# SwiGLU_1's first half in staircase order, with the first root's Newton steps on GpSimd

## The chip, the cores and the metric

The kernel runs as one program on one core of a Trainium2 chip. The metric is the device time of one execution in microseconds (us), as the median of several runs.

## The reference, cut to what matters

One decoder layer on 256 tokens of width 2048, in float32: SwiGLU_1, a mixer, SwiGLU_2, each behind an RMSNorm whose output is scaled and shifted by vectors that come from the conditioning `c` (adaLN).

```python
cond = jax.nn.silu(c)
mod = cond @ ada_w[l] + ada_b[l]                       # 2048 x 18432
sh1, sc1, gt1, ... = jnp.split(mod, 9, axis=-1)
h = rmsnorm(x, norm_g[l, 0]) * (1 + sc1) + sh1
x = x + 0.5 * gt1 * ((silu(h @ wg) * (h @ wu)) @ wd)   # wg, wu 2048 x 5632
...
```

The change touches what comes first: the norm of x, the first columns of `mod`, and the products `h @ wg` and `h @ wu` for 28 of the 44 tiles of 128 features.

## The kernel before, in words

**Weights.** All products are made of 128x128 weight tiles, which lie in HBM in the order of their use, eight to a block of 512 KB. `Stream.next` hands out the next tile. At the first tile of a block, `Stream.block` starts the block's load on SP's queue (`wraw`), ScalarE (ACT) rounds it to float32r (`whi`), and VectorE (DVE) subtracts to get the rest (`wlo`). A product in float32 is then three products in float32r: high weight by high h, high weight by low h, low weight by high h. In the first half those are the three matmuls of `three`, each with 256 columns. `raw`, `hi` and `lo` have four buffers each; every fifth block's `wraw` has a buffer of its own (`more`).

**The columns of mod.** One column of 128 outputs of `mod` is a row of 1 MB of `ada_w` (`adat`, or `adaf` for the first four), multiplied by silu(c) and summed by one DVE instruction (L257). The first two columns are done in halves (`first_col`, L683). h of contraction step k (128 of the 2048 inputs) needs two columns, scale and shift of k, and then `modulate_one` makes the high part of h on ACT and the low part on DVE, both in the tile `hs`. `Stream.next` calls `ada_col` at the pace of the table RATE (columns per block), and `ada_need` forces those that are still missing when a k is first used.

**The first half.** `gate_up_first` works on 28 pairs f; a pair is the gate tile and the up tile of one 128-wide slice of features, which share a PSUM bank of 512 columns. The pairs form groups of 8, 8, 8 and 4. Eight banks are all there is. CHUNKS splits the 16 steps of k into 0 to 1, 2 to 7 and 8 to 15, and every group goes through one chunk before the next begins. In each chunk group 0 leads: its eight pairs stand in eight banks and take the first LEAD steps k by k, so that each h is used sixteen times before the next is needed; the rest goes pair by pair. At the end of a chunk `evacuate` takes the bank: after the first chunk ACT copies it to an SBUF tile `acc` (L577), after the second DVE adds it to `acc` (L579), and after the last DVE adds gate and up (`tg`, `tu`, L582 and L583), ACT does the silu, DVE the product, and both split the result into `hid` (L497).

**The start.** Warm-up matmuls on zeros (`zp`), 32 transposes of x (`px`, copied to `x` by ACT), the squares of x on ACT, then the reciprocal root on DVE: a guess by bit shift and two Newton steps (`rsqrt`, L281 to L289). DVE spreads the two roots over `frb`, two matmuls make them a row over all partitions (`nrow`), and ACT copies it. Then h of k=0 can be made. The tiles of the start live in the pool `early`, which is closed ahead of the first half; the tiles `acc` and `hid` come from the pool that takes its place in SBUF, where the third and fourth column (`adaf`) are still to be summed.

Each engine runs its own instructions strictly in the order in which the build put them; the build's scheduler moves instructions of different steps past each other, and `tc.issue_after` binds it.

Of the kernel before, what the change touches and what calls it, by code (L numbers as in the profile page):

```python
# [30 lines left out]
GR = 24  # L31
NEG = -1e30

RATE = ((0, 0.5), (24, 0.34), (56, 0.45), (68, 0.06), (112, 0.5), (168, 0.38), (264, 0.1), (280, 0.25), (408, 0.125))
N_BIG, N_GDN = 3, 3
N_FIRST = 4
AHEAD = 4
N_WARM = (10, 7)
TILE_US = 0.35
HIDX = 3  # L40
MORE = True
# [9 lines left out]
MAGIC = 0x5F3759DF  # L51
# [37 lines left out]
class Stream:  # L89


    def __init__(self, nc, w, raw, hi, lo):
        self.nc, self.w, self.raw, self.hi, self.lo = nc, w, raw, hi, lo
        self.order = []
        self.more = None
        self.h = self.l = self.last = None
        self.owed, self.side, self.quiet = 0.0, lambda: None, False
        self.tc, self.hold, self.held = None, None, []
        self.first = []
        self.late, self.owing = False, []  # L100

    def settle(self):
# [4 lines left out]
    def behind(self, later=True):  # L107
# [2 lines left out]
            self.hold = self.held.pop(0)  # L110
        return nullcontext() if self.hold is None else self.tc.issue_after(self.hold)

    def block(self, b):

        raw, hi, lo = self.raw, self.hi, self.lo
        if self.more is not None and b % 5 == 4:
            raw = self.more
        r = raw.tile([P, WB * P], F32, name="wraw")
        self.last = self.nc.sync.dma_start(r, self.w[b]).ins
        self.h = hi.tile([P, WB * P], F32R, name="whi")  # L120
        self.cast = self.nc.scalar.copy(self.h, r).ins  # L121
        return r, lo

    def next(self, mat, k, n, width=1):
        i = len(self.order)
        if i % WB == 0:
            nc = self.nc
            b = i // WB
            r, lo = self.first.pop(0) if self.first else self.block(b)
            self.l = lo.tile([P, WB * P], F32R, name="wlo")  # L130
            pace = [r_ for r_ in RATE if r_[0] <= b][-1][1]
            with self.behind():
                nc.vector.tensor_tensor(self.l, r, self.h.bitcast(F32), ALU.subtract)  # L133
# [13 lines left out]
def layer_kernel(ctx: ExitStack, tc: tile.TileContext, xrow, c, adaw, cols, cst, w, out, order, dbg=None):  # L147
    nc = tc.nc
    V, A, G, PE = nc.vector, nc.scalar, nc.gpsimd, nc.tensor
# [26 lines left out]
    W = Stream(nc, w, raw, hi, lo)  # L176
# [3 lines left out]
    x = keep.tile([P, KD, T], F32, name="x")  # L180
# [4 lines left out]
    ep = early.enter_context(tc.tile_pool(name="early", bufs=1))  # L185
# [6 lines left out]
    one = ep.tile([P, P], F32, name="one")  # L192
# [168 lines left out]
    def modulate_one(j, g1, sh, r, weave=True):  # L361

        t = pt("ht")
        hl, hh, tt = (run(j, LO), run(j, HI), turns(t)) if weave else (plain[:, j, LO], plain[:, j, HI], t)
        V.scalar_tensor_tensor(t, x[:, j], g1, r, ALU.mult, ALU.mult)
        if j % 2:
            A.activation(t, t, AF.Identity, bias=sh)
            A.copy(hh, tt)  # L368
            return V.tensor_tensor(hl, tt, hh.bitcast(F32), ALU.subtract)
        else:  # L370
            with tc.issue_after(W.cast) if W.first else nullcontext():
                A.activation(hh, tt, AF.Identity, bias=sh)  # L372
            return V.scalar_tensor_tensor(hl, tt, sh, hh.bitcast(F32), ALU.add, ALU.subtract)

    def gains(which, m_sc, j, n):
# [173 lines left out]
    def gate_up_first(fs, hp):  # L549

        r = first_row
        for j in range(KD):
            ada_done[0, j] = lambda j=j: modulate_one(j, gains(0, 1, j, 1), mod[:, j : j + 1], r)
        W.hold, W.held = None, [ada_done[0, 0]().ins]
        groups = [fs[i : i + 8] for i in range(0, len(fs), 8)]
        chunks = list(zip(CHUNKS[:-1], CHUNKS[1:]))
        acc, hids = {}, []

        def three(ps, f, s, k, k0, k1):
            o = ps[:, s * T : (s + 1) * T]  # L560
            wh, wl = W.next(("gu"[s], 0), k, f)
            first, last = k == k0, k == k1 - 1
            skip = s == 1
            PE.matmul(o, wh, part(k, HI), start=first and s == 0, stop=False, skip_group_check=skip)  # L564
            PE.matmul(o, wh, part(k, LO), start=False, stop=False, skip_group_check=skip)  # L565
            PE.matmul(o, wl, part(k, HI), start=False, stop=last, skip_group_check=skip)  # L566

        turn = [0]

        def bank():  # L570
            turn[0] += 1
            return psn(turn[0], "pgu")

        def evacuate(ps, f, ci):
            if ci == 0:
                acc[f] = hp.tile([P, 2 * T], F32, name="acc", tag="hid")
                A.copy(acc[f], ps)  # L577
            elif ci < len(chunks) - 1:
                V.tensor_add(acc[f], ps, acc[f])  # L579
            else:  # L580
                tg, tu = pt("tg"), pt("tu")
                V.tensor_add(tg, ps[:, :T], acc[f][:, :T])  # L582
                V.tensor_add(tu, ps[:, T:], acc[f][:, T:])  # L583
                hids.append(swi(tg, tu, hp))

        for ci, (k0, k1) in enumerate(chunks):
            for gi, grp in enumerate(groups):
                if gi == 0 and LEAD[ci]:
                    pb = {f: bank() for f in grp}
                    ks = k0 + LEAD[ci]  # L590
                    for k in range(k0, ks):
                        ada_need(0, k)
                        for f in grp:
                            for s in range(2):
                                three(pb[f], f, s, k, k0, k1)
                    for f in grp:
                        for k in range(ks, k1):
                            ada_need(0, k)
                            for s in range(2):
                                three(pb[f], f, s, k, k0, k1)  # L600
                        evacuate(pb[f], f, ci)
                else:
                    for f in grp:
                        pf = bank()
                        for k in range(k0, k1):
                            ada_need(0, k)
                            for s in range(2):
                                three(pf, f, s, k, k0, k1)
                        evacuate(pf, f, ci)
        return hids  # L610

    def ffn(which, m_gt, early=None):
# [41 lines left out]
    hold = None  # L654
    for kind, i in (("x", 0), ("x", 1), ("c", 0), ("c", 1), ("x", 2), ("x", 3), ("c", 2), ("c", 3)):
        with nullcontext() if hold is None else tc.issue_after(hold):
            if kind == "c":
                hold = cond(i)
            else:
                t, q = divmod(i, 2)  # L660
# [8 lines left out]
        with tc.issue_after(hold):  # L669
            return A.copy(x[:, 2 * i : 2 * i + 2], px.rearrange("p (a t) -> p a t", a=2))  # L670

    for i in range(4):
        features(i)
    fv = ep.tile([P, 2], F32, name="fv")

    def first_col(i, q):

        hf = slice(q * D // 2, (q + 1) * D // 2)
        m, j = ada_seq[i]
        col = m * KD + j  # L680
        part = ep.tile([P, 1], F32, name=f"part{i}")
        t = first_ada[i][:, hf]
        parts[i] = V.tensor_tensor_reduce(t, t, cs[:, hf], 1.0, L("adab", col, 1) if q == 0 else parts_[i], ALU.mult, ALU.add,  # L683
                                          part if q == 0 else mod[:, col : col + 1]).ins
        if q == 0:
            parts_[i] = part
        return parts[i]

    parts, parts_ = {}, {}
    first_col(0, 0)  # L690
    V.tensor_tensor(fv, ss[:, :, 0], ss[:, :, 1], ALU.add)
    V.tensor_scalar(fv, fv, 1.0 / D, EPS, ALU.mult, ALU.add)
    fy = rsqrt(fv, [P, 2], "n")
    frb = ep.tile([P, 2, P], F32, name="frb")
    pr = psf("nrow")
    for t in range(2):
        V.tensor_scalar(frb[:, t], one, fy[:, t : t + 1], None, ALU.mult)
        nr = PE.matmul(pr[:, t * P : (t + 1) * P], frb[:, t], ident, start=True, stop=True)
    first_row = tmp.tile([P, T], F32, name="nrow", bufs=1)
    hold = A.copy(first_row, pr[:, :T]).ins  # L700
    for i in range(4, KD // 2):
# [722 lines left out]
```

## Time and profile before

| | us |
|---|---|
| three runs | 1949.29, 1952.88, 1954.36 |
| median | 1952.88 |
| the profiled execution | 1954.36 |
| its span, first to last instruction | 1952.6 |
| PE busy | 1902.9 (97%) |
| DVE busy | 1557.3 (80%) |
| ACT busy | 1035.5 (53%) |
| POOL (GpSimd) busy | 57.0 (3%) |
| matmuls of the first half, first to last start | 22.8 to 337.0 |

A row of the timeline has the start in us from the span's start, the duration, the engine, the source line, the operation, output<-input by the program's names, the shapes and a count; in brackets stands the idle time of the engine ahead of it and what ended that. PEld are weight loads, which run beside the matmuls. Matmuls are pipelined, so the time of one is the distance from start to start and not its duration.

### The profile page before, as it was taken

How to read it: one execution, taken by the hardware profiler on the slowest of the kernel's cores; microseconds unless marked ns; L12 is line 12 of the kernel's file. 1: busy time of each engine (PE TensorE's matmuls, PEld its weight loads, DVE VectorE, ACT ScalarE, POOL GpSimd, SP SyncE). 2: the span in 40 equal slices, each digit the busy share in tenths (PEclk: the TensorE clock that was granted, in tenths of full speed). 3: DMA queues.
4: the chain of work that ended last, by engine and by line, in shares of the span. 5: the costliest groups of instructions: out<-in, count | busy, mean ns of one | idle time of the engine just before them, and what ended most of it. 6: DMA issues, size and time to landing. Idle time of an engine off the chain costs nothing.

```text
span 1952.6 us, 33709 instructions
## 1 busy us (share of the span) xinstructions
PE 1902.9 (97%) x13087; PEld 1776.3 (91%) x13087; DVE 1557.3 (80%) x2415; ACT 1035.5 (53%) x1645; POOL 57.0 (3%) x55
## 2 busy tenths in 40 slices
PE   8999999999999999999999999999999999999998
PEld 6999999998999988889989998889999999999997
DVE  6999978989999997889978979886766656565654
ACT  6544554433454446857657655565554445555553
POOL 0000000000000120000000002000000000000011
PEclk8999999999999999999999999999999999999999
DMA  9989867999999986685566658676777665555553
GB/s 369 359 321 349 300 221 254 398 381 376 356 353 342 347 317 218 251 302 205 203 239 236 211 215 315 226 258 249 255 249 239 201 200 203 201 200 202 200 202 119
DMA packets 129490, 519.58 MB, mean 266 GB/s; under 512 B 18217, under 2 KB 21545, under 8 KB 111153
## 3 DMA queue, kind: packets, MB, share of 16 engines
q1 hardware_dynamic: 129330, 517.42, 72.7%
q8 instruction: 103, 1.69, 0.3%
q14 instruction: 57, 0.47, 0.1%
HBM read 512.89 MB, written 4.47 MB: 265 GB/s over the span
## 4 chain that ended last, share of the span: by engine, by line
PE 76%; DVE 11%; DMA 5%; issue 4%; ACT 3%; SPq 0%; DVEq 0%; ACTq 0%
PE pd L482 14%; PE pg L478 10%; PE pu L478 10%; PE pd L483 7%; PE pu L479 5%; PE pg L479 5%; PE pgu L566 5%; PE pgu L565 5%; PE pgu L564 5%; DVE wlo L133 4%; DMA adat<-in_ada_dram 3%; DVE adat L257 2%; PE pp L758 2%; PE pp L759 2%; PE pp L760 2%
## 5 line engine op out<-in xcount | busy, mean ns | idle before, releaser
L133 DVE TENSOR_TENSOR wlo<-wraw,whi 128x1024 fp32r<-128x1024 f32 x674 | 821.1, 1227 | 242.7 <-ACT whi L121 241.3
L121 ACT CAST whi<-wraw 128x1024 fp32r<-128x1024 f32 x674 | 700.1, 1047 | 509.3 <-PE pd L482 166.5
L482 PE MATMUL pd<-hid,whi 128*128 128x512 f32 x1408 | 461.8, 382 | 0.0
L483 PE MATMUL pd<-hid,wlo 128*128 128x256 f32 x1408 | 384.6, 273 | 2.6 <-DVE wlo L133 2.4
L257 DVE CUSTOM_DVE_ANT_0 adat<-adat,cs,colt 128x2048 f32<-128x2048 f32 x140 | 329.5, 2354 | 40.9 <-DMA adat<-in_ada_dram 40.8
L478 PE MATMUL pg<-hs,whi 128*128 128x512 f32 x912 | 302.1, 382 | 2.5 <-DVE shc L429 2.5
L478 PE MATMUL pu<-hs,whi 128*128 128x512 f32 x912 | 302.2, 382 | 0.0
L482 PEld LDWEIGHTS pd<-hid,whi 128*128 128x128 f32 x1408 | 266.0, 189 | 36.5
L483 PEld LDWEIGHTS pd<-hid,wlo 128*128 128x128 f32 x1408 | 270.3, 192 | 5.4 <-DVE wlo L133 5.3
L564 PE MATMUL pgu<-hs,whi 128*128 128x256 f32 x896 | 245.3, 277 | 6.2 <-ACT hs L368 6.2
L479 PE MATMUL pu<-hs,wlo 128*128 128x256 f32 x912 | 249.3, 273 | 0.0
L479 PE MATMUL pg<-hs,wlo 128*128 128x256 f32 x912 | 248.9, 273 | 0.0
L566 PE MATMUL pgu<-hs,wlo 128*128 128x256 f32 x896 | 245.2, 278 | 2.4 <-DVE wlo L133 2.4
L565 PE MATMUL pgu<-hs,whi 128*128 128x256 f32 x896 | 246.8, 277 | 0.0
L478 PEld LDWEIGHTS pg<-hs,whi 128*128 128x128 f32 x912 | 172.4, 189 | 26.7 <-ACT whi L121 2.7
L478 PEld LDWEIGHTS pu<-hs,whi 128*128 128x128 f32 x912 | 172.4, 189 | 23.7
L758 PE MATMUL pp<-hs,whi 128*128 128x256 f32 x656 | 188.9, 289 | 1.5 <-ACT hs L372 1.5
L760 PE MATMUL pp<-hs,wlo 128*128 128x256 f32 x656 | 182.7, 278 | 1.1 <-DVE wlo L133 1.1
L759 PE MATMUL pp<-hs,whi 128*128 128x256 f32 x656 | 182.5, 278 | 0.0
L564 PEld LDWEIGHTS pgu<-hs,whi 128*128 128x128 f32 x896 | 172.3, 193 | 6.9 <-ACT hs L368 6.6
L479 PEld LDWEIGHTS pu<-hs,wlo 128*128 128x128 f32 x912 | 175.0, 192 | 1.3 <-DVE wlo L133 1.2
L479 PEld LDWEIGHTS pg<-hs,wlo 128*128 128x128 f32 x912 | 175.1, 192 | 0.4
(337 smaller groups left out, 2583.6 us busy)
## 6 DMA issues: line engine op xcount, KB each, us to landing
wraw<-in_w_dram SPq DMA_DIRECT2D x674, 512.0 KB, 4.3
adat<-in_ada_dram SPq DMA_DIRECT2D x140, 1024.0 KB, 7.4
xr<-in_xr_dram SPq DMA_DIRECT2D x4, 512.0 KB, 5.1
adaf<-in_ada_dram SPq DMA_DIRECT2D x4, 512.0 KB, 8.7
adaf<-in_ada_dram SPq DMA_DIRECT2D x2, 1024.0 KB, 11.3
xd<-x SPq DMA_DIRECT2D x4, 512.0 KB, 5.0
rw<-rowd SPq DMA_DIRECT2D x16, 128.0 KB, 6.7
x<-xd SPq DMA_DIRECT2D x4, 512.0 KB, 5.4
```

The costliest lines, as they stand in the source:

```text
L121: self.cast = self.nc.scalar.copy(self.h, r).ins
L133: nc.vector.tensor_tensor(self.l, r, self.h.bitcast(F32), ALU.subtract)
L257: V.tensor_tensor_reduce(t, t, cs, 1.0, L("adab", q, 1), ALU.mult, ALU.add, mod[:, q : q + 1])
L478: PE.matmul(ps, wt[0], both, start=(k == 0), stop=False)
L479: PE.matmul(ps[:, T:], wt[1], part(k, HI), start=False, stop=(k == KD - 1))
L482: PE.matmul(ps, wt[0], act.rearrange("p q (a b) -> p q b a", a=2), start=first, stop=False)
L483: PE.matmul(ps[:, :T], wt[1], woven(act[:, 0]), start=False, stop=last)
L564: PE.matmul(o, wh, part(k, HI), start=first and s == 0, stop=False, skip_group_check=skip)
L565: PE.matmul(o, wh, part(k, LO), start=False, stop=False, skip_group_check=skip)
L566: PE.matmul(o, wl, part(k, HI), start=False, stop=last, skip_group_check=skip)
L758: PE.matmul(pp[i][:, :T], wh, hh, start=(k == 0), stop=False)
L760: PE.matmul(pp[i][:, :T], wl, hh, start=False, stop=(k == KD - 1))
```

## The change

It changes four things.

1. The order of the first half. PIECES replaces CHUNKS and LEAD. An entry (g, k0, ks, k1) says: group g goes from k0 to k1, with k0 to ks pair-interleaved and the rest pair by pair. Group 0 now has three pieces (k 0; 1 to 3; 4 to 15), group 1 (0 to 1; 2 to 5; 6 to 15), group 2 (0 to 2; 3 to 9; 10 to 15), group 3 two (0 to 5; 6 to 15). The work is the same; there are 28 copies to `acc`, 24 adds to it where there were 28, and 28 closings.
2. The first root. The guess stays on DVE; the two Newton steps (ten instructions of 128x2) and the spreading to `frb` go to GpSimd, and the first half columns of `mod` stand behind the guess on DVE.
3. The start's order: six instead of four copies of transposes ahead of `nrow`, four instead of seven warm-ups after it, the first block's cast in two halves with h of k=0 between them, h of k=1 made like that of even k.
4. RATE has 0.43 up to block 70 instead of 0.5, 0.34 and 0.45.

```diff
-CHUNKS = (0, 2, 8, 16)
-LEAD = (2, 5, 5)
+PIECES = (
+    (0, 0, 1, 1), (1, 0, 2, 2), (2, 0, 3, 3), (0, 1, 4, 4), (1, 2, 6, 6), (3, 0, 0, 6),
...
-RATE = ((0, 0.5), (24, 0.34), (56, 0.45), (68, 0.06), ...
+RATE = ((0, 0.43), (70, 0.06), ...
-N_WARM = (10, 7)
+N_WARM = (10, 4)
...
     # Stream.block
-        self.cast = self.nc.scalar.copy(self.h, r).ins
+        with nullcontext() if b != 1 else self.tc.issue_after(self.lead):
+            one, *more = self.pieces(b)
+            h = self.h
+            self.cast = self.nc.scalar.copy(h[:, one], r[:, one]).ins
+            self.rest = [lambda q=q: self.nc.scalar.copy(h[:, q], r[:, q]) for q in more]
...
     # modulate_one
-        V.scalar_tensor_tensor(t, x[:, j], g1, r, ALU.mult, ALU.mult)
-        if j % 2:
+        with tc.issue_after(parts[1]) if W.first else nullcontext():
+            V.scalar_tensor_tensor(t, x[:, j], g1, r, ALU.mult, ALU.mult)
+        if j % 2 and j > 1:
...
     # gate_up_first
-        for ci, (k0, k1) in enumerate(chunks):
...
+        for g, k0, ks, k1 in PIECES:
+            grp = fs[8 * g : 8 * g + 8]
+            pb = {f: bank() for f in grp} if ks > k0 else {}
+            for k in range(k0, ks):
+                ada_need(0, k)
+                for f in grp:
+                    for s in range(2):
+                        three(pb[f], f, s, k, k0, k1)
+            for f in grp:
+                if f not in pb:
+                    pb[f] = bank()
+                for k in range(max(k0, ks), k1):
+                    ada_need(0, k)
+                    for s in range(2):
+                        three(pb[f], f, s, k, k0, k1)
+                evacuate(pb[f], f, k0, k1)
...
     # the start
-    for i in range(4):
+    for i in range(KD // 2 - 2):
         features(i)
...
-    first_col(0, 0)
-    fy = rsqrt(fv, [P, 2], "n")
+    V.tensor_scalar(fa.bitcast(I32), fv.bitcast(I32), 1, None, ALU.logical_shift_right)
+    guess = V.tensor_scalar(fy.bitcast(I32), fa.bitcast(I32), -1.0, float(MAGIC), ALU.mult, ALU.add)
+    with tc.issue_after(guess.ins):
+        first_col(0, 0)
+    for c0, c1, c2 in ((0.0, -0.1875, 0.5625), (64.0 / 9.0, -10.0 / 3.0, 5.0)):
+        G.tensor_tensor(fa, fy, fy, ALU.mult)
+        G.tensor_tensor(fa, fa, fv, ALU.mult)
...
+        G.tensor_tensor(fy, fy, fa, ALU.mult)
...
-        V.tensor_scalar(frb[:, t], one, fy[:, t : t + 1], None, ALU.mult)
+        G.tensor_scalar(frb[:, t], one, fy[:, t : t + 1], None, ALU.mult)
...
-    W.first.append(W.block(0))
+    with tc.issue_after(hold):
+        W.first.append(W.block(0))
```

How the instructions move, at three places. First PE at the start, from the row of roots (`nrow`) on; `px` are transposes of x, `zp` warm-ups. Before:

```order
L698 MATMUL nrow<-colt,frb 128x128 x2
L668 MATMUL px<-colt,xr 128x128 x8
L198 LDWEIGHTS zw
L198 MATMUL zp<-zw 128x512
L198 LDWEIGHTS zw
```

Now:

```order
L720 MATMUL nrow<-colt,frb 128x128 x2
L675 MATMUL px<-colt,xr 128x128 x4
L210 LDWEIGHTS zw
L210 MATMUL zp<-zw 128x512
L210 LDWEIGHTS zw
L210 MATMUL zp<-zw 128x512
L210 LDWEIGHTS zw
L210 MATMUL zp<-zw 128x512
L210 LDWEIGHTS zw
L210 MATMUL zp<-zw 128x512
L675 MATMUL px<-colt,xr 128x128 x4
L579 MATMUL pgu<-hs,whi 128x256 x2
```

The last four transposes now stand behind the warm-ups and right ahead of the first products; before, all eight stood ahead of the seven warm-ups.

Second ACT, from the casts of the first blocks to the copies of group 0's banks into `acc`, with h of k=1 (`hs`) among them; `whi` are the casts of the blocks in their order. Before:

```order
L121 CAST whi_329<-wraw_327 128x1024
L121 CAST whi_359<-wraw_357 128x1024
L367 ACTIVATE ht_322<-ht_322,mod_126 128x256
L368 CAST hs_127<-ht_322 128x2x128
L577 COPY acc_390<-pgu_252 128x512
L121 CAST whi_409<-wraw_407 128x1024
L577 COPY acc_392<-pgu_253 128x512
```

Now:

```order
L131 CAST whi_377<-wraw_375 128x1024
L131 CAST whi_415<-wraw_413 128x1024
L592 COPY acc_319<-pgu_254 128x512
L592 COPY acc_321<-pgu_255 128x512
L592 COPY acc_323<-pgu_256 128x512
L592 COPY acc_325<-pgu_257 128x512
L592 COPY acc_327<-pgu_258 128x512
L592 COPY acc_329<-pgu_259 128x512
L592 COPY acc_331<-pgu_260 128x512
L592 COPY acc_333<-pgu_261 128x512
L385 ACTIVATE hs_127<-ht_409,mod_126 128x2x128
L131 CAST whi_448<-wraw_446 128x1024
```

Group 0's eight copies have moved ahead of h of k=1. In the built program the first of them waits for DVE's total of the fourth column (besides PE's products), since its tile lies in the SBUF that the column was loaded to, and PE's first product of group 1 waits for that copy.

Third DVE, at the closing of group 0, whose pairs are now pgu_1885 to pgu_1892; `wlo_2659` and `wlo_2707` are the blocks 68 and 69 of the weights, and `wlo_2759`, thirteen small rows further on, is block 70. Before, with the pairs pgu_2216 to pgu_2223:

```order
L133 TENSOR_TENSOR wlo_2647<-wraw_2643,whi_2645 128x1024
L133 TENSOR_TENSOR wlo_2695<-wraw_2691,whi_2693 128x1024
L582 TENSOR_TENSOR tg_2586<-pgu_2216,acc_390 128x256
L583 TENSOR_TENSOR tu_2587<-pgu_2216,acc_390 128x256
L133 TENSOR_TENSOR wlo_2734<-wraw_2730,whi_2732 128x1024
L513 TENSOR_TENSOR tu_2587<-tu_2587,tg_2586 128x256
L582 TENSOR_TENSOR tg_2622<-pgu_2217,acc_392 128x256
L583 TENSOR_TENSOR tu_2623<-pgu_2217,acc_392 128x256
```

Now, from the closing of pgu_1888 (pair 3) on:

```order
L597 TENSOR_TENSOR tg_2646<-pgu_1888,acc_325 128x256
L514 TENSOR_TENSOR hid_2601<-tu_2596,hid_2601 128x256
L530 TENSOR_TENSOR tu_2626<-tu_2626,tg_2625 128x256
L598 TENSOR_TENSOR tu_2647<-pgu_1888,acc_325 128x256
L145 TENSOR_TENSOR wlo_2659<-wraw_2655,whi_2657 128x1024
L514 TENSOR_TENSOR hid_2631<-tu_2626,hid_2631 128x256
L530 TENSOR_TENSOR tu_2647<-tu_2647,tg_2646 128x256
L145 TENSOR_TENSOR wlo_2707<-wraw_2703,whi_2705 128x1024
L514 TENSOR_TENSOR hid_2652<-tu_2647,hid_2652 128x256
L269 ISA adat_2709,mod_126<-adat_2709,cs_86,colt_87 128x2048
L269 ISA mod_126 128x1
L597 TENSOR_TENSOR tg_2673<-pgu_1889,acc_327 128x256
```

Before, the blocks stood between the closing steps of single pairs, two ahead of the first; now blocks 68 and 69 stand behind those of four pairs, and block 70 behind those of all eight. In PE's order `wlo_2659` is first used in matmul 1640 of the half and `wlo_2759` in matmul 1684, counted from 0; the last products of pgu_1888 and pgu_1892 are matmuls 1631 and 1679.

More of the change, by code (lines that the diff above doesn't have):

```diff
@@ L132, in next @@
             with self.behind():
[L133 removed]
+                for q in self.pieces(b):
+                    nc.vector.tensor_tensor(self.l[:, q], r[:, q], self.h[:, q].bitcast(F32), ALU.subtract)
             self.settle()
@@ L371, in modulate_one @@
             with tc.issue_after(W.cast) if W.first else nullcontext():
-                A.activation(hh, tt, AF.Identity, bias=sh)
+                i = A.activation(hh, tt, AF.Identity, bias=sh)
+            if W.first:
+                W.lead = i.ins
+                with tc.issue_after(W.lead):
+                    W.rest.pop()()
             return V.scalar_tensor_tensor(hl, tt, sh, hh.bitcast(F32), ALU.add, ALU.subtract)
@@ L584, in evacuate @@
                 hids.append(swi(tg, tu, hp))
-        for ci, (k0, k1) in enumerate(chunks):
[L587 to L609, printed above, removed]
+        for g, k0, ks, k1 in PIECES:
[14 more added lines that the diff above has]
+                evacuate(pb[f], f, k0, k1)
         return hids
@@ L689, in layer_kernel @@
     parts, parts_ = {}, {}
-    first_col(0, 0)
     V.tensor_tensor(fv, ss[:, :, 0], ss[:, :, 1], ALU.add)
     V.tensor_scalar(fv, fv, 1.0 / D, EPS, ALU.mult, ALU.add)
-    fy = rsqrt(fv, [P, 2], "n")
+    fy = ep.tile([P, 2], F32, name="fy")
+    fa = ep.tile([P, 2], F32, name="fa")
+    V.tensor_scalar(fa.bitcast(I32), fv.bitcast(I32), 1, None, ALU.logical_shift_right)
[5 more added lines that the diff above has]
+        G.tensor_tensor(fa, fa, fv, ALU.mult)
+        if c0:
+            fb = ep.tile([P, 2], F32, name="fb")
+            G.tensor_scalar(fb, fa, c0 * c0, c0 * c1, ALU.mult, ALU.add)
+            G.tensor_tensor(fa, fa, fb, ALU.mult)
+            G.tensor_scalar(fa, fa, c2, None, ALU.add)
+        else:
+            G.tensor_scalar(fa, fa, c1, c2, ALU.mult, ALU.add)
+        G.tensor_tensor(fy, fy, fa, ALU.mult)
     frb = ep.tile([P, 2, P], F32, name="frb")
@@ L700, in layer_kernel @@
     hold = A.copy(first_row, pr[:, :T]).ins
-    for i in range(4, KD // 2):
+    for i in range(KD // 2 - 2, KD // 2):
         features(i)
```

16 lines of the change are left out of this document (10 added, 6 removed).

## The prediction

> **What bounds the kernel now.** I first asked for the busy time of each engine in four stretches, cut where the first half of SwiGLU_1 begins and ends. The columns are the stretch, its length, busy time and instructions of PE, PEld, DVE, ACT and POOL, the granted clock, the DMA share and GB/s.
>
> ```profile
> 0.00:22.70 22.70, 17.76 (x60) 10.43 (x61) 8.22 (x27) 13.98 (x26) 0.22 (x4) 0.78 0.91 351
> 22.70:106.40 83.70, 75.39 (x630) 74.06 (x628) 75.83 (x86) 47.68 (x68) 0.00 (x0) 0.96 0.91 355
> 106.40:337.40 231.00, 230.69 (x2062) 230.48 (x2063) 207.32 (x283) 112.17 (x151) 0.00 (x0) 1.00 0.79 290
> 337.40:1952.60 1615.20, 1579.02 (x10338) 1461.36 (x10336) 1265.93 (x2023) 861.67 (x1402) 56.81 (x51) 1.00 0.71 257
> ```
>
> TensorE bounds this kernel: from 106.4 to 337.4 it idles 0.3 us. What the change can win lies ahead of 106.4; what it can lose lies in all of the first half. The timeline of PE gives the pace and the waits.
>
> ```profile
> 299.81 0.28 PE L566 MATMUL pgu<-hs,wlo 128*128 128x256 f32 x1
> 310.53 0.28 PE L566 MATMUL pgu<-hs,wlo 128*128 128x256 f32 x1
> 32.35 0.49 PE L564 MATMUL pgu<-hs,whi 128*128 128x256 f32 x2 [3.89 <-ACT hs L368]
> 97.27 0.73 PE L564 MATMUL pgu<-hs,whi 128*128 128x256 f32 x4 [2.33 <-ACT hs L368]
> 106.47 0.38 PE L566 MATMUL pgu<-hs,wlo 128*128 128x256 f32 x1 [1.47 <-DVE wlo L133]
> ```
>
> Between the first two rows lie 96 matmuls, so one takes 0.1117 us, a weight tile (three of them) 0.335 and a block of eight tiles 2.68. The half has 896 tiles, 2688 matmuls; I number them from 0 in the order of PE. Matmuls 0 to 627 need 70.1 us at this pace and took 83.7, so 13.6 us are lost, in three waits (3.9, 2.3, 1.5) and the clock behind them. The clock is in the same matmuls by stretches of 2 us (busy PE, granted clock, DMA):
>
> ```profile
> 94.00:96.00 2.00, 0.93 (x9) 1.00 0.98 406
> 96.00:98.00 2.00, 0.73 (x5) 0.96 0.57 231
> 98.00:100.00 2.00, 2.00 (x12) 0.50 0.86 287
> 100.00:102.00 2.00, 2.00 (x14) 0.69 1.02 410
> ```
>
> After a wait of 2.33 us the clock is halved for about 3.4 us, which costs another 1.7. The Trainium skill, page "TensorE: Matmul & The Clock Gate", Part 1, has the clock fall only after an idle window of about 3.4 us; this trace differs, 2.33 us were enough. By the page the wait of 2.7 us below costs no clock, by the row it may cost 1.7; the sum is the same, since the longer wait right behind it takes that up.
>
> **The start.** Now the timeline up to the first product.
>
> ```profile
> 11.96 0.17 DVE L281 TENSOR_SCALAR rsa_n<-fv 128x2 int32<-128x2 int32 x1
> 12.09 1.28 DVE L683 CUSTOM_DVE_ANT_0 adaf<-adaf,cs,colt 128x1024 f32<-128x1024 f32 x1
> 17.08 0.48 DVE L697 TENSOR_SCALAR frb<-one,rsy_n 128x128 f32<-128x128 f32 x2
> 18.43 1.91 PE L668 MATMUL px<-colt,xr 128*128 128x128 f32 x8
> 18.68 0.37 ACT L700 COPY nrow<-nrow 128x256 f32<-128x256 f32 x1 [4.24 <-PE nrow L698]
> 18.95 1.57 ACT L670 COPY x<-px 128x512 f32<-128x512 f32 x3
> 20.14 2.96 PE L198 MATMUL zp<-zw 128*128 128x512 bf16 x7
> 21.80 0.56 ACT L372 ACTIVATE hs<-ht,mod 128x256 fp32r<-128x256 f32 x1
> 22.40 0.48 DVE L373 SCALAR_TENSOR_TENSOR hs<-ht,mod,hs 128x256 fp32r<-128x256 f32 x1 [2.83 <-ACT hs L372]
> ```
>
> Today `frb` is ready at 17.56, and h of k=0 (its high part, ACT at 21.80) ends 4.8 us later. The Newton steps now go to POOL, while DVE runs the four half columns (L683) back to back behind the guess. How POOL and DVE share is in the later rows where both work:
>
> ```profile
> 721.85 2.34 DVE L257 CUSTOM_DVE_ANT_0 adat<-adat,cs,colt 128x2048 f32<-128x2048 f32 x1
> 722.59 2.20 POOL L310 TENSOR_TENSOR sqacc<-sqacc,sq 128x256 f32<-128x256 f32 x1 [3.78 <-ACT sq L306]
> 724.18 1.69 DVE L133 TENSOR_TENSOR wlo<-wraw,whi 128x1024 fp32r<-128x1024 f32 x1
> 734.55 0.73 POOL L310 TENSOR_TENSOR sqacc<-sqacc,sq 128x256 f32<-128x256 f32 x1 [5.03 <-ACT sq L306]
> 750.93 0.12 POOL L961 MEMSET x<- 64x16 f32 x1
> 669.32 1.19 POOL L310 TENSOR_TENSOR sqacc<-sqacc,sq 128x256 f32<-128x256 f32 x1 [668.87 <-ACT sq L306]
> L310 POOLq MODIFY_POOL_CONFIG  x2: 11/11/11, 0.8 to 0.8; - x2
> ```
>
> Alone, POOL's add takes 0.73. The one at 722.59 meets a column on DVE and ends at 724.79, 0.6 after the column does, and DVE's next instruction takes 1.69 where it takes 1.14 otherwise: POOL waits out DVE's instruction, then DVE waits out POOL's. So each of the dependent Newton steps that meets a half column waits for its end: one step per half column. DVE: guess done at 12.3, four half columns of 1.21 and three holds of 0.3 end at 18.0. POOL has then done 4 of 10 steps; 6 more at 0.25 (a bare MEMSET is 0.12, the large add 0.73; I take a value near the small one, plus the step's own wait) and two `frb` at 0.35 (half the elements of the 0.73 row) end at 20.2, against 17.56: 2.7 later. The rest of the path grows as well. PE now has four transposes (0.95), four warm-ups (4 x 0.42) and then the last four transposes (0.95) between the row sum and h, and ACT copies both results (0.52 each) and casts half a block (0.5) ahead of h: 6.1 us behind `frb` instead of 4.8, 1.3 later. **Start: +4.0.** Lower end, with no holds and 0.2 a step: -1.4. Upper end, with 0.73 for each of the eight instructions left: +7.7.
>
> The Trainium skill, page "GPSIMD Engine Reference", "Instruction dispatch", adds about 6 us to the first call of a freshly loaded kernel, without a record. The first add here (669.32) shows nothing of it, and the two loading instructions stand at 0.8. By the page the sum would be up to 6 us higher, if the load starts only with the first step.
>
> **From h of k=0 to matmul 628.** I count from the row at 22.40; matmul 628 (the row at 106.47) comes 84.1 after it. The durations:
>
> ```profile
> 72.83 2.35 DVE L133 TENSOR_TENSOR wlo<-wraw,whi 128x1024 fp32r<-128x1024 f32 x2
> 75.10 2.35 DVE L257 CUSTOM_DVE_ANT_0 adat<-adat,cs,colt 128x2048 f32<-128x2048 f32 x1
> 77.37 0.08 DVE L257 DVE_READ_ACCUMULATOR2_ANT mod<- 128x1 f32 x1
> 38.64 2.05 ACT L577 COPY acc<-pgu 128x512 f32<-128x512 f32 x4
> 101.31 3.98 DVE L579 TENSOR_TENSOR acc<-pgu,acc 128x512 f32<-128x512 f32 x6 [0.38 <-PE pgu L566]
> 105.20 1.22 DVE L133 TENSOR_TENSOR wlo<-wraw,whi 128x1024 fp32r<-128x1024 f32 x1
> 219.15 0.41 DVE L582 TENSOR_TENSOR tg<-pgu,acc 128x256 f32<-128x256 f32 x1
> 219.49 0.41 DVE L583 TENSOR_TENSOR tu<-pgu,acc 128x256 f32<-128x256 f32 x1
> ```
>
> From start to start, a `wlo` block costs DVE 1.14, an ada column 2.27, an acc add 0.65, a 128x256 step 0.34; an acc copy costs ACT 0.5. In the staircase PE does group 0 with k=0 (matmuls 0 to 47) and then turns to group 1. All eight PSUM banks hold group 0, so matmul 48 waits for ACT's first acc copy. That copy also waits for the fourth ada column's total: the acc tiles lie where the closed pool `early` kept the third and fourth column. ACT's row no longer has h of k=1 ahead of the copies, as before. DVE reaches that total after h 0.4, two half blocks 1.2, two blocks 2.3, a column 2.27, g and ht 0.5, a block 1.14 and the column 2.27: 10.1. With the copy, PE goes on at 10.7; it had finished its 48 matmuls at 5.7. So the wait of 3.9 for k=1 becomes one of 5.0 for a bank, with 1.7 of clock behind it. The next h come in time. Two bursts of eight acc adds remain. Pair 0 of group 0 is done with matmul 389; then DVE has an add 0.65, a column 2.27, seven adds 4.55 and a block 1.2, 8.7 in all, while PE has 67 matmuls (7.5) until matmul 456 needs that block: 1.2. From there to the `wlo` that matmul 628 needs, DVE has 1.1 + 14.0 (three columns, five blocks, 1.5 of small steps) + 5.6 (eight adds, an h) + 1.2 = 21.9 and PE 172 matmuls, 19.2: 2.7. Together 10.7 + 1.7 + 580 x 0.1117 + 1.2 + 2.7 = 81.1 instead of 84.1. **This part: -3.0**, between -8.6 (clock and both bursts free) and +2 (a halved clock behind the last wait, and 3 more for DVE).
>
> **The end of group 0.** Group 0 now closes with two k per pair, 12 matmuls or 1.34 us, where it had three, 2.0 us; DVE's closing steps of a pair (four of 0.34) and two thirds of a block (0.57) no longer fit. The order of DVE (in the part on the change) shows what gives: the `wlo` that matmul 1640 needs stands behind the steps of pair 3, whose last product is matmul 1631, and the one that matmul 1684 needs behind pair 7, done with matmul 1679. First: 0.28 for the product, four steps 1.34, the block 1.2, less eight matmuls without `wlo` (0.9): 1.9, and 2.7 with ACT's silu and casts that DVE waits for between. Second: from block to block DVE has sixteen steps 5.4, a column 2.27 and two blocks 2.3, 9.9 in all, PE 44 matmuls 4.9: 5.0, and 5.5 with ACT's part. Then 1.7 of clock. Before, these stretches had no wait (the window from 106.4). **+9.9**, at least 6.9. From matmul 1708 on DVE stays ahead, and all behind the first half is the same work.
>
> **Edits with one answer.** Casting block 0 in halves and fusing h of k=1 is inside the sums. RATE only shifts columns, 32 of which are due by block 66 in both; DMA, at 0.91 busy, would have to bring 0.97 MB per 2.68 us, 362 GB/s, of which 355 are shown, so columns stay just in time (0; if not, up to 2).
>
> **The sum**: 4.0 - 3.0 + 9.9 = +10.9. On the profiled execution that is 1954.36 + 10.9 = 1965.3 (span 1952.6 + 10.9); it is the slowest of the three shown, so I set it against their median, 1952.88: **1963.8**.
>
> **Rivals.** (1) No one is held: POOL's steps slip between DVE's accesses, the start comes 1.4 earlier, the bursts and the clock cost nothing (-8.6), the end of group 0 costs its least with the clock (8.6): -1.4, 1951.5. For it: steps of two elements may need the port too briefly to be held; against it, the whole 0.6 after each column above. (2) The staircase does all it looks like (faster): if h of k=1 and the banks come by the time PE asks, all 13.6 us go and only the least of the closing wait, 6.9, comes: -6.7, 1946.2. It turns on the fourth column's total at 5.7 after the first h; DVE's row has 10.1 of work ahead of it, and only an order other than the one built would change that. (3) POOL is slower still: eight instructions at 0.73, +3.7 more: 1967.5, and with the upper ends of the second part 1972.
>
> **How the numbers follow.** About 0.3%, 5.9 us, is what a measurement can tell from no change. The forecast has 0.60, rival 3 0.14, rival 1 0.17, rival 2 0.09. The first two are slower, rival 1 is the same, rival 2 faster: 0.74, 0.17, 0.09. The range goes from 1954, which leaves out rival 2 and half of rival 1, to 1972.
>
> **What would show it.** Right: POOL's steps ending just behind the half columns, `frb` near 20, the first product near 26.5; the second wait of PE at matmul 48 on an acc copy; two waits of 2 to 6 us on `wlo` about 200 us after, with a halved clock. Wrong: `frb` by 16, PE not idle between groups 0 and 1, or a busy PE through the closing of group 0.

## The result, and the profile after

The changed kernel takes 1978.22 us (median of 4 runs, 1973.6 to 1980.55), the kernel before 1952.54 beside it: a ratio of 1.0132, 95% interval 1.0115 to 1.0148, or +25.7 us. Forecast were slower and +10.9. The profiled execution after took 1980.55 us, span 1978.7, against 1954.36 and 1952.6.

The stretches of the changed kernel, cut at the first product, at matmuls 628 and 1708 and behind the half (stretch, length, busy PE, PEld, DVE, ACT, POOL, granted clock, DMA share, GB/s):

```profile
0.00:25.90 25.90, 18.40 (x58) 10.95 (x58) 6.84 (x17) 13.48 (x26) 7.18 (x16) 0.73 0.92 361
25.90:105.30 79.40, 73.93 (x628) 73.34 (x628) 74.29 (x88) 45.17 (x63) 0.00 (x0) 0.96 0.87 330
105.30:236.50 131.20, 123.75 (x1080) 123.34 (x1081) 124.06 (x155) 60.26 (x79) 0.00 (x0) 0.98 0.85 334
236.50:345.90 109.40, 109.40 (x980) 109.40 (x979) 83.15 (x125) 54.41 (x78) 0.00 (x0) 1.00 0.67 240
345.90:1978.70 1632.80, 1589.01 (x10343) 1472.59 (x10341) 1264.96 (x2021) 860.03 (x1399) 57.47 (x51) 0.99 0.70 254
```

The same two stretches of the kernel before, from matmul 628 on:

```profile
106.40:227.60 121.20, 120.89 (x1080) 120.70 (x1081) 117.97 (x147) 55.15 (x67) 0.00 (x0) 1.00 0.89 338
227.60:336.90 109.30, 109.30 (x982) 109.30 (x981) 88.84 (x137) 56.52 (x84) 0.00 (x0) 1.00 0.67 238
```

From h of k=0 (DVE's low part, below) to matmul 628 it is 79.4 us where it was 84.1; the 1080 matmuls behind it take 131.2 us instead of 121.2; the rest of the half is practically equal (109.4 and 109.3). The half ends 9.1 us later. The other 17 us lie behind it: 1632.8 us where the kernel before has 1615.7 (1952.6 less 336.9). Nearly all of them are in the mixer, and they are spread over it: with PE's matmuls matched one by one, the changed kernel is 9.4 us behind at 750 us of the kernel before, 15.0 at 850, 18.0 at 1150, 26.1 at 1330, and 26.1 from there to the end. In windows over the same work, first of the kernel before and then of the changed one:

```profile
747.00:1300.00 553.00, 530.91 (x3947) 501.18 (x3948) 480.97 (x1052) 358.82 (x726) 15.83 (x18) 0.99 0.67 238
```

```profile
757.00:1327.00 570.00, 540.73 (x3951) 512.40 (x3952) 483.94 (x1054) 357.33 (x722) 16.30 (x18) 0.97 0.65 231
```

For practically the same matmuls PE idles 29.3 us instead of 22.1 and is busy 9.8 us longer at a lower granted clock (0.97 for 0.99): 7 us of waiting and 10 of clock. Other waits head the list (engine, line, releaser, sum, times, longest), before and after:

```profile
PE po L1089 <- DVE st L1100: 3.4, 3, 1.9
PE po L483 <- DVE wlo L133: 3.2, 2, 2.4
PE pg L478 <- DVE shc L429: 2.5, 1, 2.5
PE pvq L1004 <- ACT kk L930: 2.5, 1, 2.5
```

```profile
PE pvq L1027 <- ACT qv L934: 7.7, 3, 4.5
PE nsum L332 <- ACT sq L318: 3.0, 2, 1.8
PE pp L783 <- DVE wlo L145: 2.4, 2, 1.9
PE po L1115 <- DVE vz L1113: 2.4, 2, 1.9
```

In the half itself PE waits where the forecast put it: at matmul 48 for an acc copy, at 628, 1640 and 1684 for `wlo` (the blocks 26, 68 and 70).

```profile
37.03 0.38 PE L579 MATMUL pgu<-hs,whi 128*128 128x256 f32 x1 [2.45 <-ACT acc L592]
105.37 0.38 PE L581 MATMUL pgu<-hs,wlo 128*128 128x256 f32 x1 [2.94 <-DVE wlo L145]
221.24 0.38 PE L581 MATMUL pgu<-hs,wlo 128*128 128x256 f32 x1 [2.48 <-DVE wlo L145]
231.31 0.58 PE L581 MATMUL pgu<-hs,wlo 128*128 128x256 f32 x1 [4.89 <-DVE wlo L145]
```

The start, POOL's row, then h of k=0:

```profile
12.28 1.22 POOL L706 TENSOR_TENSOR fa<-fy 128x2 f32<-128x2 f32 x1 [11.83 <-DVE fy L702]
13.58 0.20 POOL L707 TENSOR_TENSOR fa<-fa,fv 128x2 f32<-128x2 f32 x1
13.87 1.06 POOL L714 TENSOR_SCALAR fa<-fa 128x2 f32<-128x2 f32 x1
...
16.41 1.25 POOL L707 TENSOR_TENSOR fa<-fa,fv 128x2 f32<-128x2 f32 x1
17.75 0.19 POOL L710 TENSOR_SCALAR fb<-fa 128x2 f32<-128x2 f32 x1
...
18.91 1.20 POOL L719 TENSOR_SCALAR frb<-one,fy 128x128 f32<-128x128 f32 x2
25.41 0.52 ACT L385 ACTIVATE hs<-ht,mod 128x256 fp32r<-128x256 f32 x1
25.97 0.48 DVE L390 SCALAR_TENSOR_TENSOR hs<-ht,mod,hs 128x256 fp32r<-128x256 f32 x1 [4.08 <-ACT hs L385]
```

A step that starts 0.09 us or more behind the start of a half column takes 1.05 to 1.25 us, until about its end, the others 0.19 to 0.22. The Trainium skill, page "SBUF — State Buffer", section "Who interferes with whom", says that DVE and GpSimd share a port pair as an exclusive lock which the first holds for its whole instruction; the long steps fit that. The step at 15.01 does so less well: by the profile it starts 0.02 behind a half column (14.99) and still takes 0.20.

### The profile page after: what moved, and what is told of

Read it like the earlier page. It is cut to its first block, busy times and chain, and to the rows that moved or that the text cites. A ratio compares the mean times of both kernels' runs of the same rounds, so it can differ in the third digit from the quotient of the medians.

```text
span 1978.7 us, 33720 instructions
## 1 busy us (share of the span) xinstructions
PE 1914.5 (97%) x13084; PEld 1789.6 (90%) x13084; DVE 1553.3 (79%) x2403; ACT 1033.4 (52%) x1641; POOL 64.7 (3%) x67
## 5 line engine op out<-in xcount | busy, mean ns | idle before, releaser
L145 DVE TENSOR_TENSOR wlo<-wraw,whi 128x1024 fp32r<-128x1024 f32 (+1 forms) x675 | 821.3, 1225 | 259.3 <-ACT whi L131 257.1
L131 ACT CAST whi<-wraw 128x1024 fp32r<-128x1024 f32 (+1 forms) x674 | 697.8, 1045 | 547.3 <-PE pd L499 166.0
L581 PEld LDWEIGHTS pgu<-hs,wlo 128*128 128x128 f32 x896 | 173.4, 195 | 11.2 <-DVE wlo L145 11.1
```

The lines of the kernel that those rows point to most:

```text
L131: self.cast = self.nc.scalar.copy(h[:, one], r[:, one]).ins
L145: nc.vector.tensor_tensor(self.l[:, q], r[:, q], self.h[:, q].bitcast(F32), ALU.subtract)
```

## The experiments

Two questions were open: what lengthens the work behind the half, and whether the waits inside it come from where the forecast put them. The table gathers all kernels but e_cols, which leaves work out: the start of the half's last matmul but one in the profiled execution, the median of the runs, and the difference of the two, which stands for what lies behind the half. It sets one execution against a median of several, so it is good to a few us. "Old" is a kernel whose PE order behind the half is that of the kernel before, but for at most four instructions; the changed kernel's differs in some 900 places.

| kernel | half ends | median (runs) | difference | mixer's order |
|---|---|---|---|---|
| before | 336.9 | 1952.5 (4) | 1615.6 | old |
| after | 346.0 | 1978.2 (4) | 1632.2 | another |
| a_phase | 346.6 | 1967.3 (4) | 1620.7 | old |
| b_phase | 335.8 | 1965.6 (4) | 1629.8 | as after |
| c_close | 348.4 | 1963.5 (4) | 1615.1 | old |
| d_newton | 345.6 | 1961.5 (4) | 1615.9 | old |
| f_pieces | 342.5 | 1957.1 (10) | 1614.6 | old |
| g_start | 341.4 | 1957.4 (7) | 1616.0 | old |
| h_start_dve | 336.0 | 1952.8 (10) | 1616.8 | old |
| i_bind | 340.5 | 1958.5 (7) | 1618.0 | old |
| k_acc | 343.1 | 1961.0 (6) | 1617.9 | old |
| l_both | 336.3 | 1951.6 (10) | 1615.3 | old |
| o_rate | 333.6 | 1951.0 (10) | 1617.4 | old |
| q_264 | 337.5 | 1954.0 (10) | 1616.5 | old |
| q_265 | 335.6 | 1968.6 (4) | 1633.0 | a third |

In the profiled executions alone, the stretch from the half's last matmul to the end of the span takes 1610.6 to 1618.4 us in every kernel of the old order, and 1632.6 (after), 1625.0 (b_phase) and 1631.2 (q_265) in the other three.

**Behind the half: a_phase and b_phase.** The pace of RATE is added up block by block and never reset: the fraction that is left over at block 112 shifts the place of every later column. There the sum is 32.62 in the changed kernel and 30.92 in the kernel before; each edit gives one of them the other's.

```diff
# a_phase, on the changed kernel
-RATE = ((0, 0.43), (70, 0.06), ...
+RATE = ((0, 0.43), (70, 0.0195), ...
# b_phase, on the kernel before
-... (56, 0.45), (68, 0.06), (112, 0.5), ...
+... (56, 0.45), (68, 0.0986), (112, 0.5), ...
```

> The changed kernel with one number of RATE altered, 0.0195 instead of 0.06 from block 70, so that the sum of the pace at block 112 is 30.92 columns as in the kernel before (it was 32.62). PE's order behind the first half is then that of the kernel before again. Theory 1: the 17 us behind the first half come from the order in which the mixer was built, which the columns' places shift; they go, and the time is about 1961 (1957 to 1965), with the first half still 9 us longer than before. Rival: they come from what the first half leaves behind at run time (a clock once lowered, late transfers); the time stays at 1978 (1974 to 1981).

> The kernel before with one number of RATE altered, 0.0986 instead of 0.06 from block 68, so that the sum at block 112 is 32.62 as in the changed kernel; PE's order behind the first half becomes that of the changed kernel, and the first half keeps its own. Theory 1 (order of the mixer): 1952.5 + 17 = about 1969 (1964 to 1973), with PE's waits of the changed kernel in the mixer. Rival (what the first half leaves behind): unchanged, 1952.

a_phase: 1967.3 (1959.1 to 1968.6), 10.9 below the changed kernel, but above its range. b_phase: 1965.6, 1.0072 of the kernel before (1.0044 to 1.0099), +12.0, with its old half and the changed kernel's head of the list: `pvq` waits 6.5 us in three waits. Theory 1 holds in both directions: one number of RATE moves the time while the half stays, so what the half leaves behind at run time is not the main part. The 5 us by which a_phase's difference in the table exceeds that of the kernel before are not explained; its profiled execution, the fastest of its four, does not have them (1610.6).

What counts is the place of a column, not which column stands there. Counted on DVE, column 99 stands behind block 272 in the kernel before and behind 266 in the changed one; a_phase has column 98 at 272, and b_phase column 100 at 266.

**One column alone: q_264 and q_265.** The kernel before, with one column called a few blocks early and the pace paid back at 269.

```diff
-... (168, 0.38), (264, 0.1), (280, 0.25), ...
+... (168, 0.38), (264, 1.1), (265, 0.1), (269, -0.9), (270, 0.1), (280, 0.25), ...   # q_264
+... (168, 0.38), (265, 1.1), (266, 0.1), (269, -0.9), (270, 0.1), (280, 0.25), ...   # q_265
```

> The kernel before with one column of mod (the one behind block 257) called 6 blocks earlier, at block 264, ahead of the norm at the mixer's start; all other columns keep their pace. PE's row stays that of the kernel before. If PE's order in the mixer decides: 1952.5, within 2. If any earlier column there costs DVE time ahead of the first h: 1954 to 1957.

> The same with the column called at block 265, one block later, so that DVE does it among the first h of the mixer (behind wlo 266), as in the changed kernel; the scheduler then puts some 700 of PE's instructions in the mixer in another order (not quite that of the changed kernel). If one column in that burst is the cause: 1958 to 1970, with new waits of PE in the mixer on pvq, prow or pft. If the whole shift is needed: 1952.5, within 2.

1954.0 and 1968.6 (ratios 1.0005, 0.9994 to 1.0016, and 1.0082, 1.0056 to 1.0109): one column, called one block later, makes 14.6 us. (1954.0 by itself lies in both of q_264's ranges, and the interval of its ratio includes no change.) On DVE the column stands so in a_phase, q_264, the changed kernel and q_265, in this order:

```profile
778.88 2.35 DVE L269 CUSTOM_DVE_ANT_0 adat<-adat,cs,colt 128x2048 f32<-128x2048 f32 x1
```

```profile
743.29 2.34 DVE L257 CUSTOM_DVE_ANT_0 adat<-adat,cs,colt 128x2048 f32<-128x2048 f32 x1
```

```profile
762.56 2.35 DVE L269 CUSTOM_DVE_ANT_0 adat<-adat,cs,colt 128x2048 f32<-128x2048 f32 x1
```

```profile
752.04 2.35 DVE L257 CUSTOM_DVE_ANT_0 adat<-adat,cs,colt 128x2048 f32<-128x2048 f32 x1
```

The mixer's first product starts at 759.3, 750.1, 757.7 and 748.1. In the first two kernels the column lies 20 us behind it or 7 ahead, in the last two 4 to 5 behind, among the steps that make the first h. Those 2.35 us are not the loss; with them the scheduler puts some 700 of PE's instructions up to the end of the mixer in another order. It reorders several hundred of DVE's and ACT's as well; no run changes one engine's row alone, so which of the three costs the time is open. q_265's new waits are not the expected ones: its longest is for a sum of squares, 500 us behind the column.

```profile
1258.62 0.37 PE L320 MATMUL nsum<-colt,sq 128*128 128x2 f32 x1 [7.15 <-ACT sq L306]
```

**The closing of group 0: c_close and e_cols.** Both are a_phase with one edit: another last piece, or 12 sums of columns that leave out half of their elements. e_cols so computes another result; it ran once, for its trace.

```diff
# c_close
-(0, 4, 14, 16)
+(0, 4, 12, 16)
# e_cols
-V.tensor_tensor_reduce(t, t, cs, 1.0, ...
+n = D // 2 if 20 <= i < 32 else D
+V.tensor_tensor_reduce(t[:, :n], t[:, :n], cs[:, :n], 1.0, ...
```

> As a_phase, but group 0's last piece is (0, 4, 12, 16): four steps of k per pair at the closing (24 matmuls, 2.7 us) instead of two (1.3 us). Theory: the waits at matmul 1640 and 1684 arise since DVE's closing steps of a pair and its wlo blocks take longer than PE's 12 matmuls; with 24 both go, with the halved clock behind them: 7 to 10 us below a_phase, about 1952. Rival: these blocks are late from HBM (the DMA share is 0 in two stretches of 4 us there); then the waits stay, and the time is a_phase's, 1961.

> As a_phase, but the sums of 12 columns of mod (the 21st to 32nd, all due by block 70) go over 1024 of the 2048 elements; the other half is left out of the sum, and the DMA stays. That takes some 12 x 1.1 = 13 us from DVE ahead of matmul 1708 and nothing else. Theory 2: from matmul 628 to 1708 DVE's whole backlog sets the pace (it idles 7 of 131 us there), not the closing steps of the two k per pair; then the waits at 1640 and 1684 shrink to under 1 us in all, the halved clock goes too, and the last matmul of the half starts near 337 instead of 346.6. Rival (closing is local, 12 matmuls against four DVE steps and two thirds of a block): both waits keep at least 4 of their 7.4 us, and the half ends at 343 or later.

c_close fits neither side. The wait for block 70 at 1684 is gone; that for block 68 stays, 2.91 us instead of 2.48, now at matmul 1636; and one of 2.07 for h is new at 1508. From 628 to 1708 it is 131.1 us as before.

```profile
229.01 0.38 PE L581 MATMUL pgu<-hs,wlo 128*128 128x256 f32 x1 [2.91 <-DVE wlo L145]
```

So I took DVE's whole backlog for the limit (theory 2), and e_cols refutes it. Both stretches, a_phase and e_cols, and e_cols' two waits:

```profile
105.90:237.20 131.30, 123.86 (x1081) 123.44 (x1082) 124.08 (x155) 60.24 (x79) 0.00 (x0) 0.98 0.86 334
```

```profile
107.40:240.60 133.20, 127.17 (x1080) 126.79 (x1081) 112.83 (x155) 59.38 (x79) 0.00 (x0) 0.95 0.86 327
226.02 0.58 PE L582 MATMUL pgu<-hs,wlo 128*128 128x256 f32 x1 [2.48 <-DVE wlo L145]
236.26 0.58 PE L582 MATMUL pgu<-hs,wlo 128*128 128x256 f32 x1 [3.47 <-DVE wlo L145]
```

DVE has 11 us less to do (112.8 for 124.1), idles 20 us, and the waits stay: 2.48 as in a_phase, and 3.47 of 4.89. Even the smaller second wait is not owed to the lighter DVE: d_newton (below) has the same 2.48 and 3.47 with all of DVE's work.

**Its order: i_bind.** The edit, on a_phase, calls a pair's evacuation three pairs later and binds it behind the last `wlo` called by then.

```diff
-                evacuate(pb[f], f, k0, k1)
+                late.append((pb[f], f, k0, k1))
+                while late[3:] or late and k0 == 0:
+                    evacuate(*late.pop(0))
...
     # evacuate, around the adds and the closing's tg and tu
+                with tc.issue_after(W.low):
```

> As a_phase, but the closing of a pair is emitted three pairs later and bound behind the last wlo emitted by then, so that DVE's row has 2 closing steps ahead of wlo 69 instead of 13, and 9 between 69 and 70 (there are 2 in a_phase). The work is the same. Theory 3 (the waits at 1640 and 1684 come from DVE's fixed row, in which closing steps stand ahead of the blocks that PE needs first, not from how much DVE has to do): of the 7.4 us in the two waits at least 4 go, and the half ends at 340 to 343 instead of 346.6. Rival (the last k of group 0, its columns and h, or HBM set the pace there): the waits come back elsewhere ahead of matmul 1708, and the half ends at 345.5 or later.

The half ends at 340.5, inside the range of theory 3 (the fixed order of DVE's row); of the 7.4 us in the two waits 3.5 remain, 0.53 for block 69 and 3.01 for block 70. Only a part of the gain is the closing's: from 628 to 1708 it is 127.75 us for 131.21. The rest comes ahead of 628, where the adds are bound as well (its wait is 1.14 for 2.93) and the clock stays full behind matmul 48, which it did not in a_phase. The time is 1958.5 against 1967.3.

```profile
221.07 0.38 PE L581 MATMUL pgu<-hs,wlo 128*128 128x256 f32 x1 [0.53 <-DVE wlo L145]
227.03 0.58 PE L581 MATMUL pgu<-hs,wlo 128*128 128x256 f32 x1 [3.01 <-DVE wlo L145]
```

**Each part alone: f_pieces, g_start, h_start_dve, d_newton.** f_pieces is the kernel before with `gate_up_first` and PIECES of the change; g_start is the changed kernel with the old ones and the old RATE. h_start_dve and d_newton are g_start and a_phase with this edit, which also puts the first two half columns back ahead of the root:

```diff
+    first_col(0, 0)
...
-    guess = V.tensor_scalar(fy.bitcast(I32), ...
...
-        G.tensor_tensor(fy, fy, fa, ALU.mult)
+    fy = rsqrt(fv, [P, 2], "n")
...
-        G.tensor_scalar(frb[:, t], ...
+        V.tensor_scalar(frb[:, t], ...
```

> The kernel before with the staircase (PIECES) alone: its own start, root, RATE. PE's order behind the first half is that of the kernel before. Theory 2 (DVE's backlog up to matmul 1708): DVE has 4.5 us more to do by then and idles about as much, so the half ends 5 to 8 us later than 337.0, the time is 1953.6 + 6.5 = 1960. Rival (the sum by places): -3.0 up to matmul 628 and +9.9 behind, 1960.5 as well, but with the first product at 22.4 and matmul 628 at 103.5; by theory 2 matmul 628 may come anywhere, and matmul 1708 comes at 233 to 236.

> The kernel before with the changed start alone (Newton steps on GpSimd, four warm-ups, the cast in halves), its own CHUNKS and RATE. First product near 26 instead of 22.8. By the places: all of it stays, +3.5, 1957. By theory 2: a part of it goes into stretches where PE would wait for DVE and HBM anyway (the waits of 3.9, 2.3 and 1.5 up to matmul 628), so that matmul 628 comes 1 to 2.5 us later than 106.5: 1955 to 1956.

> As g_start, but with the Newton steps and frb on DVE. First product near 20.5 (as measured with the staircase) instead of 22.8. By the places: 2.3 us earlier throughout, 1951.3. By theory 2: most of it is lost to longer waits ahead of matmul 628, which comes 0 to 1 us earlier than 106.5, and the time is that of the kernel before within 1 us.

> As a_phase, but with the root's Newton steps and frb on DVE again, as before; the rest of the changed start stays. Theory: frb ends at 17.6 instead of 20.1, and the first product and all behind it come 2.5 us earlier, 1.0 remains of the start's loss: 1958.5. Rival: the first h is held by the half columns (now later behind the Newton steps) or by ACT, not by frb: the time stays within 1 us of a_phase.

The staircase alone costs 4.2 us (1957.1, ratio 1.0017, 1.0006 to 1.0028) and 5.6 in the half; 6.5 were expected. Matmul 628 comes at 100.8 and not at 103.5, and the 1080 behind it take 130.8; there PE loses 7.0 us in five waits instead of 7.4 in two, the longest 2.04 at matmul 1708. The changed start alone costs 4.5 in time and in the half (ratio 1.0030, 1.0018 to 1.0043): all of the later first product stays. With the Newton steps on DVE the same start is even (1.0006, 0.9990 to 1.0021): its first product comes at 20.7, 2.1 earlier than before, but only 0.9 of that is left at matmul 628 and at the half's end. So here a later start costs its whole length, while an earlier one is in part lost to new waits ahead of 628. d_newton's comes at 20.49, 4.5 ahead of a_phase, more than the 2.5 expected, and meets the wait at matmul 48:

```profile
20.49 0.45 PE L579 MATMUL pgu<-hs,whi 128*128 128x256 f32 x1
...
32.31 0.58 PE L579 MATMUL pgu<-hs,whi 128*128 128x256 f32 x1 [5.30 <-ACT acc L592]
```

At the half's end 1.0 is left; the time is 1961.5, not 1958.5.

**The bank: k_acc, l_both, o_rate.** The third and fourth column come from the pool of the later ones instead of `early`, whose place the acc tiles take.

```diff
-N_FIRST = 4
+N_FIRST = 2
```

> As d_newton, but only two columns of mod in the pool early (N_FIRST 2): the first acc copy no longer waits for the fourth column's total. Forecast's step: the wait of 5.3 at matmul 48 goes to under 1; PE then has 48 matmuls of group 1 with k=0 and may wait for k=1 instead, 0 to 3 us. Matmul 628 comes 2 to 5 us earlier than d_newton's 103.0. If the loss is only moved (DVE, HBM), it is back at matmul 1708: 236 as in d_newton; if it stays, 232 to 234.

> i_bind and k_acc together (Newton steps on DVE, two early columns, closings bound behind wlo). By theory 3 the gains add: the half ends at 334 to 338, as the kernel before or 2 us earlier, and the time is 1950 to 1955. By the rival (a stretch-wide limit of DVE or HBM) the half ends at 343 or later, 1959.

> As l_both with the RATE of the kernel before (0.5, 0.34, 0.45 up to block 68), which brings three more columns ahead of block 24 and the columns behind the half to their old places. If the pace of columns up to block 70 matters for the waits of the closing, the half ends 1 to 4 us earlier than in l_both; if not, within 1 us.

In k_acc matmul 48 follows at once at 26.50, and PE waits 1.06 at 36.38. Matmul 48 comes 5.8 us earlier than in d_newton, but matmul 628, at 101.3, only 1.7 (2 to 5 were expected): the wait at 628 has grown from 2.93 to 3.73, and smaller ones are new. The half ends 2.5 earlier; the time, 1961.0, does not show it. l_both ends the half at 336.3 and takes 1951.6 (ratio 0.9997, 0.9986 to 1.0008): the gains add. o_rate, with the old pace of columns, ends it at 333.6, 2.6 ahead of l_both and 3.2 ahead of the kernel before: the pace up to block 70 bears on the closing too (from 628 to 1708 it is 125.2 us for 127.0). It takes 1951.0 (0.9991, 0.9982 to 1.0000): even with the kernel before or a trace faster. Its stretches from the first product to 628, 1708 and the last:

```profile
19.30:99.20 79.90, 76.48 (x630) 72.90 (x629) 73.66 (x85) 45.04 (x64) 0.00 (x0) 0.98 0.94 359
99.20:224.40 125.20, 122.15 (x1082) 121.03 (x1081) 117.24 (x142) 58.17 (x74) 0.00 (x0) 1.00 0.88 338
224.40:333.60 109.20, 109.20 (x980) 109.20 (x980) 87.97 (x139) 57.33 (x85) 0.00 (x0) 1.00 0.72 248
```

## Why the prediction was wrong

- **Start, +4.0: right**, +3.6 in the trace (25.97 for 22.40), +4.5 as a part of its own. POOL had six of ten steps behind it at the end of the half columns, not four, and `frb` took 0.6 each, not 0.35; it was ready at 20.1 for 20.2. That these two errors cancel is luck.
- **From h of k=0 to matmul 628, -3.0: right in kind**, -4.7. The wait at 48 was 2.45 instead of 5.0, since PE, at half clock up to 32 us, took 8.3 us over its 48 matmuls; matmul 48 came 11.1 behind that h, for 10.7. The clock stayed full behind this wait, so the 1.7 for it did not come, nor did the 1.2 at matmul 456; 628 waited 2.9 for 2.7.
- **End of group 0, +9.9: right**, +10.0, in waits of 2.5 and 4.9 for 2.7 and 5.5. i_bind shows the step itself, the fixed row of DVE with closing steps ahead of `wlo`, for about half of the two waits, and e_cols that it isn't the amount of DVE's work. That the two k per pair cause it is not borne out: with four (c_close) the wait for block 68 stays, and the stretch is as long.
- **All behind the first half, 0: wrong**, +17. This step failed: "all behind the first half is the same work" was taken for the same time. It rested on "RATE only shifts columns, 32 of which are due by block 66 in both". That count is right, and so is the work; but the pace's sum goes on with 32.62 at block 112 where it had 30.92. One of these 1.7 columns had been forced ahead of its pace in the kernel before and not in the changed one, so the later columns stand 0.7 of a place early: column 36 behind block 98 instead of 109, column 99 behind 266 instead of 272. There it falls among the first h of the mixer, and the scheduler builds the mixer in another order. The built program's rows behind block 112 show it; the prediction read them for the first half alone. Of the +25.7 some 9 are the half and 11 to 17 the mixer. That the size differs (10.9, 12.0, 14.6 and 17 by four comparisons, of which 14.6 is for a third order) is not settled; a_phase's four runs are 9.5 us apart.
- The rivals: none of them had this step. Rivals 1 and 2 (an earlier start, no waits) are refuted by the rows above; rival 3 by POOL's steps of 0.20.

## What to carry to other kernels

A pace that accumulates ties an early stage to every later one: when its early numbers change, choose them so that the later calls fall at their old places, and compare the built order behind the change as well as at it. When the order is made by a scheduler, "the same work" is no argument for the same time; here one instruction of 2.35 us, placed a few blocks elsewhere, cost 14.6. When a wait is local to an engine's fixed row, taking work off that engine need not help (e_cols), while moving the needed instruction ahead can (i_bind).

## What the runs showed of the hardware

In these traces the clock is lowered by how little PE is busy in one window of a fixed grid of 3.41 us, not by the length of a wait. All halved stretches of the first half lie on such a grid and are whole numbers of windows long. The changed kernel and c_close wait 2.94 and 2.93 us at matmul 628. In each trace's grid, first the changed kernel, then c_close:

```profile
100.43:103.84 3.41, 2.01 (x18) 1.81 (x17) 3.41 (x7) 2.09 (x2) 0.00 (x0) 1.00 0.84 353
103.84:107.25 3.41, 1.88 (x16) 1.88 (x17) 3.41 (x4) 0.00 (x0) 0.00 (x0) 1.00 0.29 88
107.25:110.67 3.42, 3.42 (x33) 3.42 (x32) 3.42 (x4) 1.83 (x3) 0.00 (x0) 1.00 0.76 271
```

```profile
104.02:107.43 3.41, 1.05 (x10) 0.86 (x8) 3.41 (x6) 1.04 (x1) 0.00 (x0) 1.00 0.53 223
107.43:110.84 3.41, 2.84 (x13) 2.84 (x14) 3.41 (x3) 0.00 (x0) 0.00 (x0) 0.50 0.49 153
```

Split over two windows, PE is busy for 2.0 and 1.9 us of each and the clock stays; within one, busy for 1.05, the next window is halved. In the sixteen profiles no window at full clock with PE busy for less than 1.5 us was followed by one at full clock, and between 1.5 and 2.0 both happened. The Trainium skill, page "TensorE: Matmul & The Clock Gate", Part 1, states the window of 3413 ns and that it runs free; the trace agrees with both, but not with the idle window of that length that it asks for: 1.9 us of idleness within a window were always enough. So, besides its own length, the same wait costs 1.7 us of clock or nothing by where it falls. That this makes the runs of one kernel differ (1947.6 to 1960.8 for the kernel before) is a guess; over the 66 runs of that kernel that list the granted clock, time and clock go together only loosely (correlation -0.37).
